# Strassen's seven products for the MLPs of a streaming encoder step

## The chip, the core and the metric

The kernel runs on one core of a Trainium2 chip. The metric is the device time of one execution in microseconds (us); lower is better. Three runs of the kernel before took 3055.25, 3056.92 and 3058.13 us. The engines are named as the profile does: PE is TensorE (matmuls), DVE is VectorE, ACT is ScalarE, POOL is GpSimd, and SP issues the DMAs.

## The reference

One step of a two-layer encoder: the first layer mixes tokens by a gated linear recurrence, the second by differential attention. Each layer ends in an MLP with a squared ReLU, and norms stand before and after each part. D is 1024, the hidden width 4096, and 1,152 tokens pass: 1,024 of a prompt and 128 of samples (8 streams of 16). All of it is fp32.

```python
def _rmsnorm(x, g):
    x32 = x.astype(jnp.float32)
    y = x32 * lax.rsqrt(jnp.mean(jnp.square(x32), axis=-1, keepdims=True) + NORM_EPS)
    return (y * g.astype(jnp.float32)).astype(x.dtype)

def _sqrelu_mlp(x, w_up, w_down):
    return jnp.square(jax.nn.relu(x @ w_up)) @ w_down
...
    for l in range(DEPTH):
        a = _rmsnorm(h, norm_g[l, 0])
...
        h = h + _rmsnorm(m, norm_g[l, 1])
        f = _sqrelu_mlp(_rmsnorm(h, norm_g[l, 2]), w_up[l], w_down[l])
        h = h + _rmsnorm(f, norm_g[l, 3])
```

## The kernel before

The 1,152 tokens are nine blocks of 128; blocks 0 to 7 are the prompt, block 8 the samples. Every large product is made of float32r pairs: an operand is split into a high part (a cast on ACT) and a low part (a subtraction on DVE), and `mm3` (L219) adds three matmuls, high by high, high by low and low by high. The normalised input of an MLP lies transposed in `aTh` and `aTl` for all nine blocks.

`out_proj` ends the mixing part: for each block in turn it adds to the residual h, takes the next norm and transposes the block (`to_aT`, four transposes into one PSUM bank, then ACT's cast and DVE's subtraction). The residual is kept in DRAM (`h_dr`).

`mlp` follows. The hidden width is 32 tiles of 128, taken in 15 groups of two or three. For each group, and for each of three groups of three token blocks, the up product `pu` is made (384 columns; L223 to L225), squared and split (L649 to L654), and then the down product `pd` of the token group before it (two halves of 512 columns in a PSUM tile of two banks) is added by DVE to an accumulator in SBUF (L618, one operation over both halves). The activations never leave SBUF. In the last group, `finish` (L622) loads h into one of three `hb` buffers, takes the norm, applies the gain on GpSimd (L629), adds (L631) and stores; in layer 0 it also takes the norm for attention and transposes.

PSUM has eight banks here: two tiles `mm`, two tiles `aux`, of a bank each, and two tiles `wide` of two banks. The order on each engine comes from a scheduler, except that the matmuls of the attention part are pinned in program order. An engine runs its instructions in that order, and each waits for semaphores of others.

Of the kernel before, what the change touches and what calls it, by code (L numbers as in the profile page):

```python
# [29 lines left out]
NFT = FF // P  # L30
EPS = 1e-6
LEVELS = (1, 2, 4, 8, 16, 32, 64)
# masked pieces of a block's scores: query offset, period and width, key range, column
# [9 lines left out]
POOL_MLP = {1, 2, 3, 4, 5, 6, 7, 8}  # L43
POOL_OUT = {4}
# attention schedule: work units between prompt steps, fill of its start, order of the parts of a step, sample parts
# [7 lines left out]
# last head: blocks whose output projection starts after a step, then the order of all blocks  # L53
# [10 lines left out]
def tile_kernel(ctx, tc, x_prompt, x_sample, cache_k, cache_v, state_hgrn, norm_g, w_hgrn_in,  # L64
# [16 lines left out]
    class Area:  # L81
        """A pool for each tag, in address order of the given tags, then of first use."""
# [6 lines left out]
        def pool(self, tag):  # L89
            if tag not in self.pools:  # L90
                self.pools[tag] = self.stack.enter_context(tc.tile_pool(name=f"{self.name}_{tag}", bufs=2, **self.kw))
            return self.pools[tag]
# [20 lines left out]
    h_dr = [dram.tile([T, D], F32, tag=f"h{i}", name=f"h_dr{i}") for i in range(3)]  # L113

    aTh = glob.tile([P, NB, KT, P], F32R, name="aTh")
    aTl = glob.tile([P, NB, KT, P], F32R, name="aTl")
    pre = ctx.enter_context(ExitStack())
# [14 lines left out]
    def load_w(src, a, n, gains=None, pool=None, sfx="", eng=None):  # L132
        """1024 elements a partition: DRAM to an exact float32r pair."""
        pool = pool or glob
        st = glob.tile([P, a, n], F32, tag="wst", name="wst", bufs=2)
# [27 lines left out]
    def rstd_of(ss, n, inv_d, pool, y=None):  # L163
        """(ss * inv_d + EPS) ** -0.5: root, reciprocal and a Newton step, scaled by powers of two."""
# [24 lines left out]

    def to_aT(a, b, psum=None, gain=None):  # L190
        """Token-major block a (SBUF) to columns of aT, times a gain of each row of a tile."""
# [17 lines left out]
    def pre_norm(h, g2, junk, dst, pool, b):  # L209
        """dst = rms-normalised h (times g2), then to aT."""  # L210
# [7 lines left out]
        to_aT(dst, b)  # L218
# [8 lines left out]
    def aT_blk(k, b):  # L227
        return aTh[:, b, k, :], aTl[:, b, k, :]
# [103 lines left out]
    with ExitStack() as hs:  # L332
# [11 lines left out]
        for h in range(H):  # L344
# [6 lines left out]
            for tg in range(NTG):  # L351
# [35 lines left out]
                # score products, level by level  # L387
# [39 lines left out]
                for c in range(3):  # L427
# [26 lines left out]
                    # token-major decayed keys  # L454
# [21 lines left out]
                    # o: sum of squares over the head, gate  # L476
# [5 lines left out]
                    # state  # L482
# [41 lines left out]
    def out_weights(w, js, gains, pp):  # L524
        """Units of an output projection: two row tiles of a half, the first half's four first."""
# [9 lines left out]
    def prepare(ob, b, o_src, osc, gain, pp):  # L535
        """Token block b of the heads' outputs, rms-normalised, to aT."""
# [11 lines left out]
    def out_proj(w, gains, gain, o_src, osc, g_post, h_old, h_new, g_pre, order, W=None, early={}):  # L548
        with ExitStack() as os_:
# [3 lines left out]

            def prep(b):
                if b not in early:
                    prepare(pp.tile([P, D], F32, name=f"ob{b % 2}", bufs=1), b, o_src, osc, gain, pp)
# [7 lines left out]
            g2 = bcast_gain(g_pre, pp, 2)  # L564
            for b in order:
# [7 lines left out]
                t = pp.tile([P, D], F32, name="t")  # L573
# [18 lines left out]
                pre_norm(hb, g2, t, t, pp, b)  # L592

# [1 line left out]
    def mlp(l, g_post, h_old, h_new, last):  # L595
# [4 lines left out]
        with ExitStack() as ms:  # L600
# [3 lines left out]
            def down(hT, wds, g, tg):  # L604
                for c in range(3):
# [13 lines left out]
                    if g == len(groups) - 1:  # L619
                        finish(b)  # L620
# [481 lines left out]
```

## Time and profile before

| | us |
|---|---|
| three runs, median | 3056.92 |
| profiled execution, span | 3055.4 |
| PE busy | 2990.4 (98%) |
| DVE busy | 1725.0 (56%) |
| ACT busy | 991.4 (32%) |
| POOL busy | 217.9 (7%) |

The span is the time of one profiled execution from its first to its last event; the busy times are how long each engine had an instruction in work, and they overlap. The stages lie so: start and recurrence to about 625 us, the first output projection to 746, MLP 0 to about 1545, attention to about 2150, its output projection to 2245, MLP 1 to about 3040, and the end.

### The profile page before, as it was taken

What the parts mean: (1) busy time and instruction counts of PE and PEld (TensorE: products, weight loads), DVE (VectorE), ACT (ScalarE), POOL (GpSimd) and SP (SyncE); (2) the same over time, 40 slices, a digit from 0 to 9 for tenths busy, and PEclk for the clock granted to TensorE, in tenths of its full rate; (3) what the DMA queues carried; (4) which work ended last, traced back from release to release, by engine and by line L of the source; (5) the groups of instructions that cost most, each with busy time, mean ns of one, the idle gap of its engine ahead of it and who ended that gap; (6) DMA issues with size and microseconds to landing.
All of it is one profiled execution on the core that took longest, in us unless ns stands there. A gap on an engine that the chain in (4) does not pass through costs nothing.

```text
span 3055.4 us, 45695 instructions
## 1 busy us (share of the span) xinstructions
PE 2990.4 (98%) x18273; PEld 2752.1 (90%) x18273; DVE 1725.0 (56%) x3418; ACT 991.4 (32%) x2376; POOL 217.9 (7%) x232
## 2 busy tenths in 40 slices
PE   7999999999999999999989999999999999999998
PEld 7999999978999999999979999997899999999997
DVE  7777777776344444444576565656653444444436
ACT  5333223333321211212254455556442212212112
POOL 1111111100000000000131020110100000000002
PEclk9999999999999999999999999999999999999999
DMA  4112121153111111111132121222431111111113
GB/s 133 52 51 58 52 58 52 58 191 111 42 41 43 42 42 42 42 42 44 61 128 75 52 85 54 69 75 64 159 117 42 42 42 42 42 42 48 36 35 110
DMA packets 227543, 199.73 MB, mean 65 GB/s; under 512 B 11865, under 2 KB 201474, under 8 KB 227330
## 3 DMA queue, kind: packets, MB, share of 16 engines
q1 hardware_dynamic: 227330, 196.81, 20.7%
q8 instruction: 144, 2.36, 0.3%
q14 instruction: 69, 0.57, 0.1%
HBM read 154.29 MB, written 42.47 MB: 64 GB/s over the span
## 4 chain that ended last, share of the span: by engine, by line
PE 92%; DVE 4%; ACT 2%; DMA 1%; issue 1%; SPq 0%; ACTq 0%; DVEq 0%
PE pj L738 9%; PE pu L223 9%; PE pu L225 9%; PE pu L224 9%; PE pd L224 8%; PE pd L225 8%; PE pd L223 8%; PE pi L223 2%; PE pi L224 2%; PE pi L225 2%; PE sc L738 2%; PE po L738 2%; PE pm L223 2%; PE pm L224 2%; PE pm L225 2%; PE pq L223 1%
## 5 line engine op out<-in xcount | busy, mean ns | idle before, releaser
L618 DVE TENSOR_TENSOR acc<-acc,pd 128x1024 f32<-128x1024 f32 x252 | 307.6, 1220 | 448.5 <-PE pd L225 448.5
L223 PE MATMUL pu<-aTh,whi 128*128 128x384 f32 x1536 | 515.4, 336 | 2.5 <-DVE aTl L206 1.8
L224 PE MATMUL pu<-aTl,whi 128*128 128x384 f32 x1536 | 514.9, 335 | 0.0
L225 PE MATMUL pu<-aTh,wlo 128*128 128x384 f32 x1536 | 514.9, 335 | 0.0
L224 PE MATMUL pd<-wlo,hh 128*128 128x512 f32 x1152 | 451.6, 392 | 0.0
L225 PE MATMUL pd<-whi,hh 128*128 128x512 f32 x1152 | 451.6, 392 | 0.0
L223 PE MATMUL pd<-whi,hh 128*128 128x512 f32 x1152 | 448.7, 390 | 1.7 <-DVE acc L618 1.7
L155 ACT CAST whi<-wst 128x1024 fp32r<-128x1024 f32 x192 | 199.0, 1051 | 603.0 <-PE pu L224 310.1
L156 DVE TENSOR_TENSOR wlo<-wst,whi 128x1024 fp32r<-128x1024 f32 x184 | 228.1, 1251 | 166.2 <-ACT whi L155 165.7
L224 PEld LDWEIGHTS pu<-aTl,whi 128*128 128x128 f32 x1536 | 288.4, 188 | 6.8
L223 PEld LDWEIGHTS pu<-aTh,whi 128*128 128x128 f32 x1536 | 288.3, 188 | 6.8 <-DVE aTl L206 2.0
L225 PEld LDWEIGHTS pu<-aTh,wlo 128*128 128x128 f32 x1536 | 288.3, 188 | 3.1
L225 PEld LDWEIGHTS pd<-whi,hh 128*128 128x128 f32 x1152 | 216.1, 188 | 45.4
L738 PE MATMUL pj<-whi,aTh 128*128 128x256 f32 x864 | 254.4, 294 | 1.9 <-DVE V L778 1.7
L223 PEld LDWEIGHTS pd<-whi,hh 128*128 128x128 f32 x1152 | 216.7, 188 | 43.4 <-DVE acc L618 2.5
L224 PEld LDWEIGHTS pd<-wlo,hh 128*128 128x128 f32 x1152 | 216.3, 188 | 41.7
L738 PE MATMUL pj<-wlo,aTh 128*128 128x256 f32 x864 | 244.9, 283 | 0.9 <-DVE wlo L156 0.9
L738 PE MATMUL pj<-whi,aTl 128*128 128x256 f32 x864 | 244.7, 283 | 0.0
L649 ACT ACTIVATE r<-pu 128x384 f32<-128x384 f32 x192 | 93.8, 489 | 414.7 <-PE pu L225 413.8
L650 DVE SCALAR_TENSOR_TENSOR r<-pu,r 128x384 f32<-128x384 f32 x192 | 106.2, 554 | 184.1 <-ACT r L649 183.8
L738 PEld LDWEIGHTS pj<-whi,aTh 128*128 128x128 f32 x864 | 165.7, 192 | 8.9 <-issue 4.5
L223 PE MATMUL pi<-whi,aTh 128*128 128x256 f32 x576 | 167.3, 290 | 1.1 <-ACT sf L365 1.1
(273 smaller groups left out, 5414.0 us busy)
## 6 DMA issues: line engine op xcount, KB each, us to landing
wst<-in_w_up_dram SPq DMA_DIRECT2D x64, 512.0 KB, 4.0
wst<-in_w_down_dram SPq DMA_DIRECT2D x64, 512.0 KB, 3.6
h_dr<-hb SPq DMA_DIRECT2D x27, 512.0 KB, 3.5
hb<-h_dr SPq DMA_DIRECT2D x27, 512.0 KB, 3.4
o_dr<-og SPq DMA_DIRECT2D x136, 64.0 KB, 1.7
wst<-in_w_hgrn_in_dram SPq DMA_DIRECT2D x16, 512.0 KB, 4.1
wst<-in_w_hgrn_in_dram SPq DMA_DIRECT2D x32, 256.0 KB, 3.0
wst<-in_w_kv_dram SPq DMA_DIRECT2D x32, 256.0 KB, 3.6
```

The source lines that it names most:

```text
L155: nc.scalar.copy(hi, st)
L156: (eng or nc.vector).tensor_tensor(out=lo, in0=st, in1=hi.bitcast(F32), op=ALU.subtract)
L223: matmul(out, lh, rh, start=first, stop=False)
L224: matmul(out, lh, rl, start=False, stop=False)
L225: matmul(out, ll, rh, start=False, stop=last)
L618: nc.vector.tensor_tensor(out=acc[b], in0=acc[b], in1=pd, op=ALU.add)
L649: nc.scalar.activation(r, pu[:, :TG], AF.Relu)
L650: nc.vector.scalar_tensor_tensor(out=r, in0=pu[:, :TG], scalar=0.0, in1=r, op0=ALU.max, op1=ALU.mult)
L738: pin(nc.tensor.matmul(*a, **k))
```

## The change

One level of Strassen's method (in Winograd's form) takes the place of the plain products for the eight prompt blocks: the operands are cut into 2 x 2 parts, seven products of sums of parts are made in place of eight, and the results are added up. Even blocks are the upper half of the tokens, odd blocks the lower; the inner width is cut in two.

- `mlp_up` has 16 iterations of two hidden tiles. Each makes P1 to P7 of 512 columns, four inner tiles by three matmuls each. P1 and P2 add up in one bank (`X`), P6, P7 and P4 in another (`Y`), P5 and P3 in half of a wide tile (`Z`). The other half of that wide tile takes the sample's product (`us`, 24 matmuls of 256 columns) and its transposes (`pt`). DVE adds u2, u3 and c22, c12, c21; ACT takes the ReLU; GpSimd squares, and the result goes to DRAM (`u_dr`, `us_dr`).
- The sums of the weights' parts are made on GpSimd (`sums`), those of the tokens' parts on GpSimd in `out_proj` (`pair_sums`); S1, S3 and S4 are transposed in the first iteration (`s_ops`), S2 takes the place of the odd blocks' first half in aT.
- `mlp_down` is a stage of its own, behind the whole of `mlp_up`. For each of 8 groups of four hidden tiles it loads the activations from DRAM, makes their sums and splits, and four token pairs by seven products of 512 columns; each product is added to its own accumulator by DVE (ACT copies in group 0). Six banks serve in turn, the last two being the halves of one wide tile. The samples' products add up in the other wide tile. Behind the last group `combine` adds the accumulators up, and `finish` works on two `hb` buffers.
- All PE work of the MLPs is pinned in program order. The weight rings are closed before an MLP and opened anew after it, pools take another mode of reuse, and `POOL_MLP` leaves GpSimd the gains of blocks 1, 3, 5, 7 and 8.

```diff
+            W = {"P1": ("A11", 0, 0, 0), "P2": ("A12", 0, 1, 0), "P3": ("S4", 0, 1, 1), "P4": ("A22", 1, 1, 0),
+                 "P5": ("S1", 1, 0, 0), "P6": ("S2", 1, 1, 1), "P7": ("S3", 1, 0, 1)}
...
+            for i in range(NFP):
...
+                X, Y, Wd = ps_mm("X"), ps_aux("Y"), ps_wide("Z")
+                Z, us, pt = Wd[:, 0:512], Wd[:, 512:768], Wd[:, 768:1024]
+                prod(X, "P1", sets, True, True)
...
+                nc.scalar.copy(p1, X)
+                if i == 0:
+                    s_ops("S1", lambda j: blk[2 * j + 1][:, 512:D])
+                sample_T(pend)
+                prod(Y, "P6", sets, True, True)
+                if i == 0:
+                    s_ops("S3", lambda j: blk[2 * j + 1][:, 0:512])
+                    s_ops("S4", lambda j: blk[2 * j][:, 512:D])
...
+                add(out=u2, in0=Y, in1=p1, op=ALU.add)
+                prod(Z, "P5", sets, True, True)
+                prod(X, "P2", sets, False, True)
...
+                nc.scalar.activation(c11, X, AF.Relu)
+                emit(c11, 0, i)
+                prod(Y, "P7", sets, False, True)
...
+                add(out=u3, in0=Y, in1=p1, op=ALU.add)
...
+                add(out=c22, in0=Z, in1=u3, op=ALU.add)
+                nc.scalar.activation(c22, c22, AF.Relu)
+                emit(c22, 3, i)
+                if nx is not None:
+                    raw = split(nx, 2 * i + 2)
+                    sums(nx)
+                wh, wl = sets[0]
+                for k in range(KT):
+                    mm3(us, aT_blk(k, NBP), (wh[:, k, :], wl[:, k, :]), k == 0, k == KT - 1, matmul)
...
+                nc.scalar.activation(hs, us, AF.Relu)
...
+                prod(Z, "P3", sets, False, True)
...
+                add(out=c12, in0=Z, in1=u2, op=ALU.add)
...
+                prod(Y, "P4", sets, False, True)
...
+                add(out=c21, in0=Y, in1=p1, op=ALU.add)
...
+            ORD = [("P1", "A11", "B11"), ("P5", "S1", "T1"), ("P7", "S3", "T3"), ("P6", "S2", "T2"),
+                   ("P2", "A12", "B21"), ("P3", "S4", "B22"), ("P4", "A22", "T4")]
...
+            def bank():
+                n = nb[0] % 6
+                nb[0] += 1
+                if n < 4:
+                    return (ps_aux if n % 2 else ps_mm)("pd")
+                if n == 4:
+                    wide[0] = ps_wide("pd")
+                return wide[0][:, (n - 4) * 512:(n - 3) * 512]
...
+                for q in range(2):
+                    mm3(o, (ah[:, q, c], al[:, q, c]), (bh[:, q], bl[:, q]), q == 0, q == 1, matmul)
+                a = ACC[p][:, j]
+                if g == 0:
+                    nc.scalar.copy(a, o)
+                else:
+                    nc.vector.tensor_tensor(out=a, in0=a, in1=o, op=ALU.add)
...
+                        combine(j)
+                        for p, an, bn in ORD[4:]:
+                            prod(g, p, an, bn, j)
+                        finish(2 * j, aE[:, :, j])
```

Where the instructions stand. In these rows a name ends in its buffer's number, and "waits" names the engine (or DMA queue) whose semaphore must have come first.

PE before, in the middle of MLP 0, where an up product gives way to the down product of the token group before (`pu_9560`, `pd_9546`; both halves of pd stand in line):
```order
L223 MATMUL pu_9560<-aTh_71,whi_9434 128x384
L224 MATMUL pu_9560<-aTl_72,whi_9434 128x384
L225 MATMUL pu_9560<-aTh_71,wlo_9435 128x384
...
L223 MATMUL pd_9546<-whi_9098,hh_9356 128x512 [waits DVE_49]
L224 MATMUL pd_9546<-wlo_9099,hh_9356 128x512
L225 MATMUL pd_9546<-whi_9098,hh_9356 128x512
```
Only the first of a down product's twelve matmuls waits there, and up matmuls stand on both sides of it.

PE of the change, in the second up iteration of MLP 0: the end of P7 (into `Y_9103`), the start and end of the sample's product and the start of P3 (both into the wide tile `Z_9104`):
```order
L218 MATMUL Y_9103<-a3h_8895,s0l_9080 128x512
L218 MATMUL Z_9104<-s2h_9025,aTh_81 128x256 [waits DVE_49]
L218 MATMUL Z_9104<-s2l_9026,aTh_81 128x256
...
L218 MATMUL Z_9104<-s2h_9025,aTl_82 128x256
L218 MATMUL Z_9104<-a4h_8925,s2h_9025 128x512 [waits Activation_49]
L218 MATMUL Z_9104<-a4l_8926,s2h_9025 128x512
```
DVE of the change, the same iteration, from u2 to c21:
```order
L763 TENSOR_TENSOR u2_9138<-Y_9103,p1_9117 128x512 [waits DVE_49,PE_49,Activation_49]
L771 TENSOR_TENSOR u3_9180<-Y_9103,p1_9117 128x512 [waits PE_49]
L773 TENSOR_TENSOR c_9182<-Z_9104,u3_9180 128x512 [waits DMAHW1_49,DVE_49]
L788 TENSOR_TENSOR c_9236<-Z_9104,u2_9138 128x512 [waits PE_49,DMAHW3_49,Activation_49,Pool_49]
L691 TENSOR_TENSOR s2l_9242<-wst0_9136,s2h_9241 128x1024 [waits Activation_49] x2
L795 TENSOR_TENSOR c_9259<-Y_9103,p1_9117 128x512 [waits DMAHW5_49,PE_49]
```
The sample's product now follows P7 at once and waits for DVE, whose c22 (`c_9182`) stands behind u3, which reads P7's bank; P3 waits for ACT.

DVE before, in MLP 0, around the accumulations of a token group (`acc0` to `acc2`):
```order
L654 TENSOR_TENSOR hh_10963<-r_10960,hh_10963 128x384 [waits Activation_49]
L618 TENSOR_TENSOR acc0_8930<-acc0_8930,pd_10966 128x1024 [waits PE_49]
L618 TENSOR_TENSOR acc1_8948<-acc1_8948,pd_10980 128x1024 [waits PE_49]
L618 TENSOR_TENSOR acc2_8966<-acc2_8966,pd_10994 128x1024 [waits PE_49]
L156 TENSOR_TENSOR wlo_11127<-wst_11124,whi_11126 128x1024 [waits DMAHW7_49,PE_49,Activation_49]
```
DVE of the change, in a middle down group, around the wide product tile `pd_12804`:
```order
L923 TENSOR_TENSOR a6_11608<-a6_11608,pd_12774 128x512 [waits PE_49]
L923 TENSOR_TENSOR a6_11608<-a6_11608,pd_12782 128x512 [waits PE_49]
L877 TENSOR_TENSOR w1l_12792<-wsta_12518,w1h_12791 128x1024 [waits Activation_49,Pool_49]
L923 TENSOR_TENSOR aE_11606<-aE_11606,pd_12804 128x512 [waits PE_49] x2
L923 TENSOR_TENSOR aE_11606<-aE_11606,pd_12819 128x512 [waits PE_49]
```
PE of the change, the two halves of that tile (the first row of each half, and what stands between):
```order
L218 MATMUL pd_12804<-w2h_12713,aTh_81 128x512 [waits DVE_49]
L218 MATMUL pd_12804<-w2l_12714,aTh_81 128x512
L218 MATMUL pd_12804<-w2h_12713,aTl_82 128x512 [waits Pool_49]
...
L218 MATMUL pd_12804<-w2h_12713,aTl_82 128x512 [waits Pool_49]
L218 MATMUL pd_12804<-w2h_12713,aTh_81 128x512 [waits DVE_49]
L218 MATMUL pd_12804<-w2l_12714,aTh_81 128x512
```
An accumulation now covers one half, a weight split (L877) stands ahead of the first half's, and the second half's first matmul waits for DVE, with nothing else on PE between the halves.

PE of the change, at the start of MLP 0, from the end of P6 to P5 (S3's and S4's transposes, `pt`; the four of a bank are two rows each):
```order
L218 MATMUL Y_8837<-aTh_81,s1l_8831 128x512
L215 MATMUL pt_8897<-ident_155,t_7731 128x128 [waits DVE_49]
L215 MATMUL pt_8904<-ident_155,t_7836 128x128 [waits DVE_49]
L215 MATMUL pt_8911<-ident_155,t_8070 128x128 [waits DVE_49]
...
L215 MATMUL pt_8948<-ident_155,t_8185 128x128 [waits DVE_49,Pool_49]
L218 MATMUL Z_8838<-a1h_8853,s1h_8830 128x512 [waits Activation_49]
```
PE before, the last block's transposes at the same point of the program (`pt_8639`, `pt_8646`), among the up matmuls:
```order
L223 MATMUL pu_8790<-aTh_71,whi_8768 128x384
L224 MATMUL pu_8790<-aTl_72,whi_8768 128x384
L196 MATMUL pt_8639<-ident_136,t_8612 128x128 [waits DVE_49,PE_49]
L196 MATMUL pt_8646<-ident_136,t_8612 128x128 [waits PE_49]
L225 MATMUL pu_8790<-aTh_71,wlo_8769 128x384
```
Before, up matmuls surround a block's transposes; now eight banks of transposes stand in one row, each waiting for DVE, and P5 behind them.

## Rows read from the trace of the kernel before

**Rows 1.** The page: the span, and the chain that ended last, by engine.
```profile
span 3055.4 us, 45695 instructions
...
PE 92%; DVE 4%; ACT 2%; DMA 1%; issue 1%; SPq 0%; ACTq 0%; DVEq 0%
```

**Rows 2.** Windows by stage: start:end, length, busy time of each engine, granted clock, DMA.
```profile
746.00:1515.00 769.00, 768.24 (x3905) 700.99 (x3905) 331.35 (x398) 170.79 (x276) 6.19 (x3) 1.00 0.14 44
1515.00:1600.00 85.00, 72.50 (x451) 64.88 (x450) 66.20 (x123) 49.43 (x99) 32.13 (x25) 0.96 0.43 138
2245.00:3015.00 770.00, 770.00 (x3918) 703.16 (x3918) 333.80 (x399) 167.75 (x273) 5.17 (x2) 1.00 0.15 44
```

**Rows 3.** The page's groups: instruction, tile, count | busy, mean ns | idle before.
```profile
L618 DVE TENSOR_TENSOR acc<-acc,pd 128x1024 f32<-128x1024 f32 x252 | 307.6, 1220 | 448.5 <-PE pd L225 448.5
...
L223 PE MATMUL pu<-aTh,whi 128*128 128x384 f32 x1536 | 515.4, 336 | 2.5 <-DVE aTl L206 1.8
...
L225 PE MATMUL pd<-whi,hh 128*128 128x512 f32 x1152 | 451.6, 392 | 0.0
```

**Rows 4.** Timeline of PE (start, length): first and last matmul of even runs; eight transposes.
```profile
1542.78 0.33 PE L223 MATMUL pu<-aTh,whi 128*128 128x384 f32 x1
...
1544.86 0.33 PE L223 MATMUL pu<-aTh,whi 128*128 128x384 f32 x1
...
1562.77 1.03 PE L196 MATMUL pt<-ident,acc 128*128 128x128 f32 x8
...
1566.15 0.39 PE L225 MATMUL pd<-whi,hh 128*128 128x512 f32 x1
...
1567.51 0.39 PE L225 MATMUL pd<-whi,hh 128*128 128x512 f32 x1
...
1570.62 0.28 PE L738 MATMUL pj<-whi,aTl 128*128 128x256 f32 x1
...
1571.93 0.28 PE L738 MATMUL pj<-wlo,aTh 128*128 128x256 f32 x1
```

**Rows 5.** Timeline of DVE and of PE: a weight split, and the matmul that waits for it.
```profile
1567.66 1.23 DVE L156 TENSOR_TENSOR wlo<-wst,whi 128x1024 fp32r<-128x1024 f32 x1 [0.25 <-ACT whi L155]
...
1568.94 0.39 PE L738 MATMUL pj<-wlo,aTh 128*128 128x256 f32 x1 [0.88 <-DVE wlo L156]
```

**Rows 6.** Groups by form: 512-element ACT cast and DVE subtraction from PSUM; GpSimd's 1,024 elements.
```profile
L206 DVE TENSOR_TENSOR aTl<-pt,aTh 128x512 fp32r<-128x512 f32 x90 | 58.9, 683 | 14.7 <-ACT aTh L205 14.7
...
L205 ACT CAST aTh<-pt 128x512 fp32r<-128x512 f32 x90 | 49.0, 587 | 43.7 <-PE pt L196 43.6
...
L629 POOL TENSOR_TENSOR acc<-acc,gb 128x1024 f32<-128x1024 f32 x16 | 39.0, 2438 | 885.1 <-ACT jk L182 885.1
```

**Rows 7.** Timeline of POOL and DVE around 1518, and the mean of that DVE operation.
```profile
1517.65 2.41 POOL L629 TENSOR_TENSOR acc<-acc,gb 128x1024 f32<-128x1024 f32 x1 [4.87 <-ACT jk L182]
...
1518.00 2.47 DVE L654 TENSOR_TENSOR hh<-r,hh 128x384 fp32r<-128x384 f32 x1 [0.25 <-ACT hh L653]
...
L654 DVE TENSOR_TENSOR hh<-r,hh 128x384 fp32r<-128x384 f32 x192 | 109.2, 570 | 92.4 <-ACT hh L653 92.2
```

**Rows 8.** Timeline of PE: two idles; the window behind the first, with its clock.
```profile
1534.03 0.50 PE L223 MATMUL pd<-whi,hh 128*128 128x512 f32 x1 [1.68 <-DVE acc L618]
...
1542.15 0.44 PE L223 MATMUL pu<-aTh,whi 128*128 128x384 f32 x1 [1.76 <-DVE aTl L206]
...
1535.00:1540.00 5.00, 4.98 (x27) 4.84 (x28) 3.93 (x7) 3.15 (x8) 0.89 (x1) 0.66 0.49 199
```

**Rows 9.** The end of the program: the last down matmul and the last DVE operation.
```profile
3040.25 0.39 PE L225 MATMUL pd<-whi,hh 128*128 128x512 f32 x1
...
3050.22 1.28 DVE L631 SCALAR_TENSOR_TENSOR hb<-acc,rs_y,hb 128x1024 f32<-128x1024 f32 x1
```

**Rows 10.** DMA issues: count, KB each, median us from issue to landing.
```profile
h_dr<-hb SPq DMA_DIRECT2D x27, 512.0 KB, 3.5
hb<-h_dr SPq DMA_DIRECT2D x27, 512.0 KB, 3.4
```

More of the change, by code (lines that the diff above doesn't have):

```diff
@@ L30 @@
 NFT = FF // P
+NFP = NFT // 2
+HT = NBP // 2 * P
 EPS = 1e-6
@@ L188, in bcast_gain, with pin, transpose, matmul @@
         return g
+    last = [None]
+    def pin(ins):
+        if last[0] is not None:
+            tc.add_manual_dep(ins.ins, last[0].name,
+                              mybir.DependencyInfo(mybir.DependencyClass.NoSync, mybir.DependencyReason.DATA),
+                              reason="order")
+        last[0] = ins.ins
+    def transpose(out, in_):
+        pin(nc.tensor.transpose(out, in_, ident))
+    def matmul(*a, **k):
+        pin(nc.tensor.matmul(*a, **k))
+    def half_T(src, hi, lo, tr=None):
+        tr = tr or (lambda o, i: nc.tensor.transpose(o, i, ident))
+        pt = ps_aux("pt").rearrange("p (k t) -> p k t", k=4)
+        for k in range(4):
+            tr(pt[:, k, :], src[:, k * P:(k + 1) * P])
+        nc.scalar.copy(hi, pt)
+        nc.vector.tensor_tensor(out=lo, in0=pt, in1=hi.bitcast(F32), op=ALU.subtract)
     def to_aT(a, b, psum=None, gain=None):
@@ L564, in out_proj @@
             g2 = bcast_gain(g_pre, pp, 2)
+            done = set()
             for b in order:
@@ L572, in out_proj @@
                     prep(todo.pop(0))
-                t = pp.tile([P, D], F32, name="t")
+                t = block(b) if b in early else blk[b]
                 if early.get(b) is not None:
@@ L662, in tile_kernel, with pair_sums @@
-    out_proj(w_hgrn_out[0], lambda kr: [gv[:, G_ON + 2 * kr + i:G_ON + 2 * kr + i + 1] for i in range(2)],
+                if b % 2 == 0:
+                    half_T(t[:, 0:512], aTh[:, b, 0:4], aTl[:, b, 0:4])
+                half_T(t[:, 512:D], aTh[:, b, 4:8], aTl[:, b, 4:8])
+                done.add(b)
+                if b < NBP and b ^ 1 in done:
+                    pair_sums(blk, b // 2)
+        return blk, keep
+    def pair_sums(blk, j):
+        e, o = blk[2 * j], blk[2 * j + 1]
+        a11, a12, a21, a22 = e[:, 0:512], e[:, 512:D], o[:, 0:512], o[:, 512:D]
+        tt = nc.gpsimd.tensor_tensor
+        tt(out=a22, in0=a21, in1=a22, op=ALU.add)
+        tt(out=a21, in0=a11, in1=a21, op=ALU.subtract)
+        tt(out=a11, in0=a22, in1=a11, op=ALU.subtract)
+        tt(out=a12, in0=a12, in1=a11, op=ALU.subtract)
+        half_T(a11, aTh[:, 2 * j + 1, 0:4], aTl[:, 2 * j + 1, 0:4])
@@ L815, in early_half @@
                 hold.append(ap.tile([P, 2, D], F32, name="KS0", bufs=1))
[L816 removed]
+                hold.extend(wr[0].tile([P, 2, 512], F32R, tag=t, name=t, bufs=NW) for t in ("whi", "wlo"))
             prepare(hold[0][:, b % 2, :], b, o_dr[1], scale_heads, gv[:, G_SUB:G_SUB + 1], ap)
```

367 lines of the change are left out of this document (283 added, 84 removed).

## The prediction

> **What bounds the kernel now.** I read the page first: its span and the chain that ended last [rows 1]. 92% of the span is TensorE (PE) on that chain, and the up products pu and the down products pd of the MLPs are the largest of its lines. Then the table of windows [rows 2]: in the two stretches in which only MLP work runs, PE is busy 768.2 of 769 us and 770.0 of 770 at a granted clock of 1.00. VectorE (DVE) has 331 to 334 us of work there, GpSimd (POOL) 5 to 6. So an MLP is paid in PE columns, and every microsecond for which PE waits in it is a microsecond of the result; PE waits for nobody there yet. The stretch behind MLP 0 is looser: PE is busy 72.5 of 85 us, 12.5 idle. Third, the timeline of PE for the price of one matmul [rows 4]: 512 columns follow each other in 1.36/6 = 0.227 us, 384 in 2.08/12 = 0.173, 256 in 1.31/11 = 0.119, and eight transposes take 1.03 us, so about (1.03 - 0.28)/7 = 0.107 each.
>
> **What the products save.** Per layer, half of the 4,608 pu and 3,456 pd matmuls (three lines of 1,536 and 1,152 each) [rows 3]: 2,304 x 0.173 + 1,728 x 0.227 = 399.3 + 391.7 = 791.0 us. After: 16 up iterations of 7 x 12 products of 512 columns and 24 sample matmuls of 256, 16 x (84 x 0.227 + 24 x 0.119) = 350.4; and 8 down groups of (28 + 4) x 6 matmuls of 512, 8 x 192 x 0.227 = 348.2. That is 698.6 a layer: **-92.4 a layer, -184.8 in all**. Only the prompt blocks lose an eighth, and the sample's 128 rows now pass alone, in 256-column and 512-column matmuls.
>
> **Transposes.** S1, S3 and S4 take 48 a layer, the sample's activations 32: 80 x 0.107 = 8.6 a layer, **+17.1**.
>
> **Waits inside an up iteration.** The sample product `us`, its transposes `pt` and P5/P3's `Z` are parts of one PSUM tile, and the order shows the first us matmul waiting for DVE and the first P3 matmul for ACT. By the numbers behind these waits, they are c22 (which reads Z) and the relu that reads us. DVE can start c22 only after u3, which needs P7's last matmul, the instruction just ahead of us on PE. Nothing else is queued on PE between them. The price: a 512-column matmul lasts 0.39 and the next could follow after 0.23, so 0.16 [rows 4]; an engine answers PE, and PE another, after about 0.05, since wlo ended at 1568.89 and pj started at 1568.94; that first matmul lasts 0.39 where a streamed one lasts 0.28, so 0.11 [rows 4, 5]; a DVE operation of 512 elements with a PSUM input takes 0.68 [rows 6]. u3 and c22: 0.16 + 0.05 + 0.68 + 0.05 + 0.68 + 0.05 + 0.11 = 1.78. The relu of 256 columns is not in the trace; ACT's 512-element cast takes 0.59 [rows 6], so it lies between 0 and 0.59, and I take 0.40, as an operation halved keeps more than half (DVE: 1.22 for 1,024, 0.68 for 512 [rows 3, 6]): 0.16 + 0.05 + 0.40 + 0.05 + 0.11 = 0.77. Together 2.55 x 32 iterations, **+81.6**. The weight splits and the sums on POOL (eight 512-element operations of about 1.2 in a 24-us iteration) stand in DVE's and POOL's order half an iteration ahead of their use, behind P3 and P1: nothing, as long as PE has those 24 us; were DVE 3 us late, P6 would wait for the rest.
>
> **Waits inside the down stage.** Products take six PSUM banks in turn; the last two are halves of one wide tile. The order has the second half's first matmul waiting for DVE (ACT in group 0), and what it waits for is the accumulation of the first half. This holds for 74 of the 448 products. Each costs 0.16 + 0.05 + 0.68 + 0.05 + 0.11 = 1.05, **+77.7**, provided that DVE is idle when the first half ends. The other four banks are four products ahead (5.4 us), which covers them.
>
> **DVE's queue in the down stage.** A group has 28 accumulations (19.0 us) and 12 splits of 1,024 elements (1.23 [rows 5]: 14.8) on DVE, 11 operations of 1,024 elements (2.44 each [rows 6]: 26.8) on POOL, against 43.6 + 4.9 of PE with the waits. So DVE is near its limit, and in 30 of the 74 places a split stands directly ahead of the accumulation that PE waits for. It starts when the accumulation before it ends, 0.9 us into a 1.36 us product, and ends 0.75 too late. What POOL adds is visible in before: a split of 384 elements that takes 0.57 lasted 2.47 when it started 0.35 us after a POOL operation, and ended with it [rows 7]. POOL is at work about half of the time here, so a split loses on average half of 2.44 with a chance of a half, 0.6. The bounds are 0 (POOL's gaps fall right) and 3.2 (0.75 and a whole POOL operation). I take 1.35 x 30 and a little carried on to the others: **+45**, between 0 and 110. The Trainium skill, page SBUF — State Buffer, section Who interferes with whom, has it that a DVE operation with two SBUF inputs and a GpSimd one that reads SBUF exclude each other for the whole instruction; the rows agree, and by it the accumulations, with one input in PSUM, stay at 0.68.
>
> **Start of each MLP.** Block 8's transposes now stand right behind P1 on PE's queue, with everything else pinned behind them. Its two norms are a chain as long as the one that ends the program (3040.6 to 3051.5 [rows 9], 10.9 us), which today runs beside pu products of other blocks. P1 covers 12 x 0.227 = 2.7, so about 8 idle. Behind P6, the eight transpositions for S3 and S4 share a single PSUM bank, as Y holds the other, so each waits for the DVE split of the last: 0.60 + 0.05 + 0.59 + 0.05 + 0.68 + 0.05 = 2.0, eight times 16, of which 3.4 is counted as transposes: 12 more. S1's four add 1 or so. **+42** for both layers, between 20 (half of the chain hidden) and 50.
>
> **From MLP 0 to attention.** Nine blocks are finished through two hb buffers instead of three, and a buffer's turn is a load (3.4), the final operation (1.28) and the store (3.5) [rows 9, 10], 8.2 us. The ninth's turn comes four turns after the first's, 33 us. Counted from where the last group's P6 ends, the first final operation comes at about 9 (12 products' third, 4.1, then square sum, gain and root), the ninth at 42, and its norm and transposes are done at 48. PE has 72 matmuls of 0.227 there and 72 transposes, 24 us, so 24 idle instead of 12.5; the order puts the first pj behind the transposes of all nine blocks. Less the waits counted already (4), and with the query weights that then load one after another (3.4 + 2.4 + 1.2 + 1.2 = 8) and a lower clock after idling: **+25**, between 5 and 45. **End of the program:** the same two buffers without norms: the ninth block's final operation ends at 43 and its store 4 later; PE's 72 matmuls and four waits end at about 20.5, so 26.5 instead of 15 (3040.3 to 3055.4 [rows 1, 9]): **+11.5**.
>
> **Sum.** 3055.4 - 184.8 + 17.1 + 81.6 + 77.7 + 45 + 42 + 25 + 11.5 = 3170.5 in the profile's terms. The median of the runs shown, 3056.92, is 1.5 above that profile's span: **3172**, slower by 3.8%.
>
> **The rivals.** *The waits are short: faster.* The gain and the transposes leave 167.7 to spend, and the boundaries (42 + 25 + 11.5) take 78.5 of it. If PE's waits inside the two stages cost under 89 us in all instead of 81.6 + 77.7 + 45 = 204, so less than half, the kernel is faster; with none it ends at 2968. For it: the boundaries are short, and each wait is for one instruction. Against it: 0.68 is what every 512-element DVE operation with a PSUM input took, and the up iteration has two in a row. Chance 0.10.
> *The clock falls at each wait.* In before, PE idled 1.68 us ahead of 1534.03, and the 5 us from 1535 on ran at a mean clock of 0.66 of full speed (1.2 GHz for part, 2.4 for the rest) [rows 8]: 1.7 us lost. After the idle of 1.76 at 1542.15 the matmuls kept their 0.173 [rows 4, 8]. If each up iteration lost 1.5 so, +48: 3220. The page TensorE: Matmul & The Clock Gate of the Trainium skill, section A second HAM failure mode, tells of a kernel whose PSUM banks in rotation made PE idle often enough for the clock to swing; the two idles here disagree on it. Chance 0.12.
> *DVE and POOL set the pace of the down stage.* If each of the 12 splits waited for a whole POOL operation, DVE's group would be 19 + 12 x 3.7 = 63 us against 51 for PE with its waits: 16 x 12 = 190 more than with a DVE that keeps up, in place of my 45: 3317. POOL's gaps speak against it. Chance 0.06.
> *The waits stand, the rest is hidden:* no queue on DVE and half of the boundaries, 3172 - 45 - 39 = 3088. Chance 0.12.
>
> **Numbers.** The forecast itself gets 0.60; its own range is 3110 to 3215. For 8 in 10 the range takes in the hidden case and the clock: 3085 to 3255. A change within 0.2%, about 6 us, is what a measurement of this kernel can't tell from none; no case ends there, 0.02 for it. Faster 0.10, slower 0.88.
>
> **What would show it.** In the changed profile, 32 idles of about 1.8 us ahead of us with DVE c22 (L773) as releaser and 32 of 0.8 ahead of P3 with ACT hs; 74 idles of 1.05 and more ahead of pd, released by acc at L923; split rows (L877, L845) above 1.23 in the mean; some 20 us idle around each MLP's first iteration; a tail of 26 us. If pd or us follow at 0.23 without a wait, the first rival is true; if matmuls of 512 columns are 0.43 apart after the waits, the clock; if POOL is busy over 80% in the down stage, the third. What would prove me wrong beyond these is an up or down window whose PE busy time is not 350 or 348.

## The result and the profile after

The changed kernel takes 3366.14 us (four runs, 3364.57 to 3368.29) against 3056.16, a ratio of 1.101 with a 95% interval of 1.0996 to 1.1028: slower by 10%, where 3172 was forecast and 3255 was the upper end of the range. The sign was right, the size was not.

The page of the kernel after, the span and the engines' line:

```profile
span 3363.0 us, 44867 instructions
...
PE 2955.6 (88%) x16897; PEld 2535.5 (75%) x16897; DVE 1976.7 (59%) x3604; ACT 1198.1 (36%) x2536; POOL 1117.2 (33%) x746
```

PE is idle for 407 us (3363.0 - 2955.6), where it was idle for 65 in the span of before [rows 1]. The product work is down by about what was forecast, but busy time counts a matmul's length, which grows when the clock falls, so it hides that here. The table of windows shows where the time goes (columns: stretch, length, busy time of PE, PEld, DVE, ACT, POOL, granted clock, DMA share, GB/s):

```profile
761.00:808.00 47.00, 25.10 (x94) 18.39 (x93) 22.00 (x30) 14.31 (x25) 13.05 (x8) 0.63 0.18 56
808.00:1209.00 401.00, 365.14 (x1732) 297.34 (x1732) 135.86 (x144) 121.29 (x176) 191.09 (x144) 0.99 0.28 91
1209.00:1224.00 15.00, 4.19 (x12) 2.65 (x11) 7.20 (x5) 6.35 (x8) 12.80 (x7) 0.64 0.69 243
1224.00:1640.00 416.00, 359.70 (x1462) 281.92 (x1460) 277.20 (x287) 129.01 (x145) 216.81 (x89) 0.96 0.23 74
1640.00:1713.00 73.00, 35.05 (x111) 25.73 (x109) 49.60 (x89) 30.06 (x57) 16.70 (x8) 0.66 0.27 90
1713.00:1800.00 87.00, 66.68 (x493) 64.20 (x493) 39.03 (x93) 37.37 (x78) 20.95 (x23) 0.81 0.28 88
3302.00:3363.00 61.00, 21.75 (x74) 16.19 (x72) 44.51 (x72) 12.75 (x28) 18.18 (x8) 0.70 0.39 138
```

The reader is to set these beside [rows 2]. The even stretches, 808 to 1209 (up) and 1224 to 1640 (down), have PE at work for 91% and 86% of the time at a clock of 0.99 and 0.96. The edges are worse: the first up iteration (761 to 808), the change from up to down (1209 to 1224), and the last group with the nine finishes (from 1640 on) have PE at work for about half of the time or less, at a clock of 0.63 to 0.66. The waits of PE, grouped by what it waited for (us in all, times, longest):

```profile
PE Z L218 <- DVE c L773: 55.0, 32, 4.1
...
PE pd L218 <- DVE a L923: 49.8, 28, 3.5
...
PE pd L218 <- DVE aO L923: 48.0, 22, 5.2
...
PE pt L222 <- ACT aO L253: 26.1, 4, 8.2
...
PE pd L218 <- DVE aE L923: 23.8, 16, 2.6
...
PE smp L218 <- ACT aTh L886: 21.3, 2, 10.7
...
PE pt L235 <- DVE t L578: 20.4, 2, 13.4
...
PE Z L218 <- ACT hs L783: 16.8, 32, 0.5
...
PE pt L222 <- POOL t L656: 16.1, 2, 9.1
```

The two waits that the forecast is built on are there: 32 for c22 and 32 for hs (71.8 us idle; with the restarts 81.6 was forecast), and 66 for DVE's accumulation of a half (121.6 us idle; 77.7 + 45 was forecast for 74 with their restarts, of which ACT releases eight). The others, 16 to 26 us each, stand at the edges. One iteration in the timeline of PE (start, length, and in brackets the idle time ahead):

```profile
1017.96 0.40 PE L218 MATMUL Y<-a3h,s2l 128*128 128x512 f32 x1
...
1019.92 0.39 PE L218 MATMUL Z<-s1h,aTh 128*128 128x256 f32 x1 [1.56 <-DVE c L773]
...
1022.74 0.28 PE L218 MATMUL Z<-s1h,aTl 128*128 128x256 f32 x1
...
1023.55 0.50 PE L218 MATMUL Z<-a4h,s1h 128*128 128x512 f32 x1 [0.53 <-ACT hs L783]
```

P7's last matmul starts at 1017.96; the sample's first would follow at 1018.19 and starts at 1019.92. P3 follows the sample's last by 0.81 instead of 0.12. Thirty such iterations took 25.15 us each, from P7 to P7; 24.66 was forecast (21.90, two transposes of 0.107 and 2.55 of waits). In the down stage, from the same view:

```profile
1406.18 0.39 PE L218 MATMUL pd<-w0h,aTl 128*128 128x512 f32 x1
...
1409.37 0.50 PE L218 MATMUL pd<-w0h,aTh 128*128 128x512 f32 x1 [2.80 <-DVE a L923]
...
1418.92 0.40 PE L218 MATMUL pd<-w2h,aTl 128*128 128x512 f32 x1
...
1421.87 0.79 PE L218 MATMUL pd<-w2h,aTh 128*128 128x512 f32 x1 [2.56 <-DVE aE L923]
...
1422.46 0.63 PE L218 MATMUL pd<-w2l,aTh 128*128 128x512 f32 x1
1422.89 0.63 PE L218 MATMUL pd<-w2h,aTl 128*128 128x512 f32 x1
```

Between halves lie 3.2 and 2.95 us here, and after the second the matmuls last 0.63 and follow at 0.43: the clock is at 1.2 GHz for a while. A group took 55.1 us (the mean from the first product of the first group to that of the eighth); 51.2 was forecast. The groups of instructions behind it:

```profile
L923 DVE TENSOR_TENSOR a<-a,pd 128x512 f32<-128x512 f32 x168 | 112.3, 682 | 76.3 <-PE pd L218 76.1
...
L877 DVE TENSOR_TENSOR w0l<-wsta,w0h 128x1024 fp32r<-128x1024 f32 x34 | 62.5, 1839 | 18.3 <-ACT w0h L876 18.3
...
L877 DVE TENSOR_TENSOR w0l<-wstb,w0h 128x1024 fp32r<-128x1024 f32 x10 | 25.2, 2516 | 6.2 <-ACT w0h L876 6.2
...
L845 POOL TENSOR_TENSOR aTl<-hst,aTh 128x1024 fp32r<-128x1024 f32 x48 | 120.9, 2521 | 88.2 <-ACT aTh L844 88.2
...
L830 POOL TENSOR_TENSOR hst<-hst 128x1024 f32<-128x1024 f32 x16 | 50.2, 3140 | 27.9 <-DVE aTl L845 27.9
...
L835 POOL TENSOR_TENSOR hst<-hst 128x1024 f32<-128x1024 f32 x16 | 38.3, 2391 | 39.3 <-DVE aTl L845 39.3
```

An accumulation, with one input in PSUM, keeps its 0.68. A split with both inputs in SBUF takes 1.47 to 2.52 in the mean of its row, 1.75 over all 192, instead of 1.23 [rows 5]. GpSimd's own sums take 2.38 to 3.14, where its gain took 2.44 [rows 6].

### The profile page after: what moved, and what is told of

It is laid out like the page before. It is cut to its first block, busy times and chain, and to the rows that moved or that the text cites. A ratio compares the mean times of both kernels' runs of the same rounds, so it can differ in the third digit from the quotient of the medians.

```text
span 3363.0 us, 44867 instructions
## 1 busy us (share of the span) xinstructions
PE 2955.6 (88%) x16897; PEld 2535.5 (75%) x16897; DVE 1976.7 (59%) x3604; ACT 1198.1 (36%) x2536; POOL 1117.2 (33%) x746
## 5 line engine op out<-in xcount | busy, mean ns | idle before, releaser
L725 POOL TENSOR_TENSOR c<-c 128x512 f32<-128x512 f32 x128 | 184.4, 1440 | 348.6 <-ACT c L789 147.7
L218 PE MATMUL pd<-w2h,aTh 128*128 128x512 f32 x304 | 131.8, 434 | 48.8 <-DVE aO L923 17.5
L262 PE MATMUL pi<-wlo,aTh 128*128 128x256 f32 x576 | 166.1, 288 | 0.0
L218 PEld LDWEIGHTS pj<-wlo,aTh 128*128 128x128 f32 x864 | 164.7, 191 | 1.8 <-DVE wlo L170 1.1
L263 PE MATMUL pi<-whi,aTl 128*128 128x256 f32 x576 | 165.4, 287 | 0.0
L218 PE MATMUL pd<-w1h,aTh 128*128 128x512 f32 x288 | 121.6, 422 | 49.6 <-DVE aO L923 25.1
L218 PEld LDWEIGHTS pj<-whi,aTl 128*128 128x128 f32 x864 | 164.4, 190 | 0.0
L218 PE MATMUL pd<-w0h,aTh 128*128 128x512 f32 x304 | 124.3, 409 | 32.1 <-DVE a L923 18.9
L218 PE MATMUL pd<-w2h,aTl 128*128 128x512 f32 x304 | 127.8, 420 | 0.0
L218 PE MATMUL pd<-w2l,aTh 128*128 128x512 f32 x304 | 127.8, 420 | 0.0
```

The lines of the kernel that those rows point to most:

```text
L218: pin(nc.tensor.matmul(*a, **k))
L262: matmul(out, lh, rl, start=False, stop=False)
L263: matmul(out, ll, rh, start=False, stop=last)
L725: nc.gpsimd.tensor_tensor(out=c, in0=c, in1=c, op=ALU.mult)
```

## Experiments

The single edits and the first two combinations were run once each. Stages that an edit leaves alone differ by 3 to 4 us between these runs (MLP 1 with the end took 941.8 us in the changed kernel, 938.5 and 938.4 in two runs whose edits lie ahead of it), so a gain below 10 us is read from the waits and not from the time alone.

**The waits inside the stages.** First the sample's own PSUM tile in the up stage:

```diff
-                Z, us, pt = Wd[:, 0:512], Wd[:, 512:768], Wd[:, 768:1024]
+                Z = Wd[:, 0:512]
...
+                Ud = ps_wide("us")
+                us, pt = Ud[:, 0:256], Ud[:, 256:512]
```

> Only the up stage changes: the sample's product and its transposes get a wide PSUM tile of their own, so they no longer share one with P5 and P3. Theory A (PE is the bound and each wait on the shared tile is paid in full): the 55 us behind DVE c22 and the 17 us behind ACT hs disappear, with some 0.1 us of restart for each of 64, so about 80 us less: 3285 us. Theory B (DVE, ACT and GpSimd set the pace of an up iteration and the shared tile only shows it): PE waits elsewhere in the iteration instead, and no more than 30 us are gained: 3335 or more.

Measured: 3275.2 us, 91 less. An iteration takes 22.51 us instead of 25.15; its products and two transposes alone were worked out at 19.04 + 2.86 + 0.21 = 22.11. Both waits are gone, and nothing took their place; the 0.40 that is left over lies in the distance of the matmuls, 0.231 to 0.234 us in the mean for 512 columns, not 0.227. Theory A.

Then five banks, each a tile of its own (the fifth is half of a wide tile whose other half stays unused), in the down stage:

```diff
-                n = nb[0] % 6
+                n = nb[0] % 5
...
-                if n == 4:
-                    wide[0] = ps_wide("pd")
-                return wide[0][:, (n - 4) * 512:(n - 3) * 512]
+                return ps_wide("pd")[:, 0:512]
```

> Only the down stage changes: five PSUM banks in turn, each a tile of its own, in place of four and two halves of a wide tile. Theory A (the wait between the halves is the loss): the 62 waits of 122 us in all disappear, the clock of 0.96 in the down stage returns to nearly 1, about 140 us less: 3225 us. Theory B (DVE and GpSimd, which exclude each other, set the pace of the down stage): PE then waits at the next reuse of a bank instead, and no more than 40 us are gained: 3325 or more.

Measured: 3220.3 us, 146 less; a group takes 44.3 us instead of 55.1. A window in the middle of that stage:

```profile
1230.00:1540.00 310.00, 310.00 (x1351) 253.36 (x1350) 248.12 (x263) 122.15 (x136) 215.86 (x79) 1.00 0.28 93
```

PE is at work all the time at a clock of 1.00, beside DVE at 80% and POOL at 70%. DVE and GpSimd did not set the pace: the splits are as long there as before (1.42 to 2.58 us in the mean by row), but with five banks in turn PE doesn't wait for them. Theory A. One thing got worse: from the last sample product of MLP 0 to the run of attention's products 116 us pass, 99 in the changed kernel.

To price the long splits, the down stage without the eight sums a group on GpSimd; three of them here, and the other five likewise:

```diff
                     x, y, z = hst["A11"], hst["A21"], hst["A22"]
-                    gp(out=x, in0=x, in1=y, op=ALU.subtract)
-                    gp(out=y, in0=y, in1=z, op=ALU.add)
                     hst["S3"], hst["S1"] = x, y
...
-                    gp(out=x, in0=hst["A22"], in1=x, op=ALU.subtract)
```

> The down stage without its eight sums a group on GpSimd (operands are split as they are loaded, so the products are of unsummed parts); GpSimd keeps three splits a group. Theory A: DVE's splits fall from means of 1.5 to 2.5 us to about 1.25, and the wait between halves from 1.9 us to some 1.1, so about 50 us less: 3315 us. Theory B: DVE and GpSimd no longer collide, the down stage runs at PE's pace, 100 us or more less: 3265 or below.

Measured: 3328.7 us, 37 less; a group takes 52.7 us instead of 55.1. The waits of PE:

```profile
PE pd L218 <- DVE aO L915: 38.2, 22, 5.1
...
PE pd L218 <- DVE a L915: 32.0, 28, 1.6
...
PE pd L218 <- DVE aE L915: 23.2, 16, 2.3
```

They fall from 121.6 to 93.4 us. That is nearer to theory A, and theory B fell. So the sums are worth about a quarter of the wait between the halves. The splits fell from 1.75 to 1.56 us in the mean over all 192, not to 1.25 as theory A had it, as three splits a group stay on GpSimd: what all of the collision is worth, no run shows.

Both PSUM edits together:

> The first two edits together (a wide tile of its own for the sample in the up stage, five single banks in the down stage). Theory A: the gains add, about 220 us less: 3145 us, still above the kernel before (3056). Theory B: 3290 or more.

Measured: 3135.8 us, 230 less, where the two had given 91 and 146 alone. They add but for 7 us. What is left, 79 us above the kernel before, lies at the edges.

**The edges, one by one.** S3's and S4's transposes ahead of the tile Y, so that they have both banks:

```diff
                     s_ops("S1", lambda j: blk[2 * j + 1][:, 512:D])
+                    s_ops("S3", lambda j: blk[2 * j + 1][:, 0:512])
+                    s_ops("S4", lambda j: blk[2 * j][:, 512:D])
                 sample_T(pend)
+                Y = ps_aux("Y")
                 prod(Y, "P6", sets, True, True)
-                if i == 0:
-                    s_ops("S3", lambda j: blk[2 * j + 1][:, 0:512])
-                    s_ops("S4", lambda j: blk[2 * j][:, 512:D])
```

> Only the first up iteration of each MLP changes: S3 and S4 are transposed right behind S1, before the bank Y is taken, so that the transposes have two banks in turn instead of one. Theory A (one bank makes each transpose wait for DVE's split of the last): of the 20 us of such waits in both layers most disappear, with the clock about 25 us less: 3342 us. Rival (the stage waits for GpSimd's sums and the norms of the last blocks anyway, so the wait only moves): within 6 us of 3366.

Measured: 3343.4 us, 23 less, theory A.

The buffers hb, from the four of the activations' loads:

```diff
-                hb = R.tile([P, 2, 512], F32, name="hb", bufs=2)
+                hb = L.tile([P, 2, HT], F32, tag="hst", name="hb", bufs=4)
```

> Only the end of each MLP changes: hb takes the four buffers of the activations' loads, which are free by then, instead of two of its own. Theory A (the turn of two buffers, load, last operation, store, sets the pace of the nine finishes): from the last group's end to the end of the program 61 us become 45, from MLP 0 to attention 97 become 70, about 43 us less: 3323 us. Rival (ACT's and DVE's order, one block behind the other, sets the pace): 3355 or more.

Measured: 3352.0 us, 14 less. It is all at the end of the program: from the last sample product to the end 47 us instead of 61, where theory A had 45. Ahead of attention 95 us were measured instead of 99, where it had a gain of 27: something else sets the pace of the finishes there.

The first sample product behind P1's products:

```diff
-                    if bn[0] == "B":
+                    if bn[0] == "B" and (g or bn != "B11"):
...
                             prod(g, p, an, bn, j)
+                        if g == 0:
+                            sample(g, bn)
```

> Only the first down group changes: its P1 products stand ahead of the first sample product instead of behind it. Theory A (the 10.6 us idle between the stages is the way of the last sample tile through DRAM, which the prompt products do not need): four products of 1.36 us move into the idle time, 11 us less in both layers: 3355 us. Rival (the prompt's activations come back from DRAM as late): within 4 us of 3366.

Measured: 3348.9 us, 17 less; PE's wait for the sample's split falls from 10.65 to 5.5 us a layer. From the last P4 to the second group the two layers gain 9 us together; where the other 8 lie, this edge doesn't explain. Theory A.

All five, and the move of the statistics tiles:

> All five edits (own wide tile for the sample, five single banks, two banks for S3 and S4, four hb buffers, P1 ahead of the first sample product), and the small statistics tiles of the first output projection moved in memory, away from the last store of the sample states. Theory A (each wait is paid by itself): 3136 of the two edits measured together, less 25, 43, 11 and 8: 3049 us, level with the kernel before. Rival (the waits behind these take their place): 3110 or more.

Measured: 3098.3 us, between the two: 37 less than with the two edits, where the other four gave 63 one by one (23, 14, 17 and, in a run further down, 9). The waits of PE in this run:

```profile
PE pt L222 <- ACT aE L253: 46.6, 4, 18.1
...
PE pt L222 <- ACT aO L253: 20.6, 4, 6.7
```

A single wait of 18.1 us, for the copy (L253) of a finished block ahead of its transposes. On PE these transposes stand ahead of the next pair's down products, so the products wait for a chain of two norms. That is what the buffers had not changed, and it is longer with five banks, 116 us as in the run with them alone; why, no run shows. The edit that follows from it, alone:

```diff
-                    for c in range(2):
-                        half_T(y[:, c], aTh[:, b, 4 * c:4 * c + 4], aTl[:, b, 4 * c:4 * c + 4])
+                    later.append((b, y))
...
             finish(NBP, a1[:, 0:2])
+            for b, y in later:
+                for c in range(2):
+                    half_T(y[:, c], aTh[:, b, 4 * c:4 * c + 4], aTl[:, b, 4 * c:4 * c + 4])
```

> Only the end of MLP 0 changes: the transposes of the nine finished blocks are written behind all nine finishes, so that none stands ahead of a down product on PE. Theory A (PE's order puts a block's transposes ahead of the next pair's products, so products wait for a chain of two norms of some 18 us, three times): the 97 us between the last group and attention become about 60, 35 us less: 3331 us. Rival (the two hb buffers set the pace of the nine finishes, whatever PE does): 3358 or more.

Measured: 3348.7 us, 17 less: a part of that edge, 87 us instead of 99, not the whole. The products no longer wait for transposes, but the nine last operations still follow each other at 7.7 us in the mean (9.2 in the changed kernel). Neither theory holds whole: the time lies between the two, and with four buffers, in the next combination, the mean is 7.6, so the buffers don't set it.

The statistics tiles of the first output projection alone (the order string of its memory begins with "ss ss8 rs_v rs_y rs_t"):

> Only the memory order of the first output projection changes: its small statistics tiles no longer lie where the sample states of the last head are stored from. Theory A (the 13.4 us idle ahead of the first output projection's transposes is DVE waiting for that store): 5 to 13 us less: 3357 us. Rival (the loads of the first blocks, late behind the first load of the up weights on SP's queue, set it): within 3 us of 3366.

Measured: 3357.1 us, 9 less. PE's wait falls from 13.4 to 6.1 us. Gone is DVE's wait for the store, which the changed kernel shows so:

```profile
641.43 0.32 DVE L183 TENSOR_SCALAR rs_v<-ssh 128x8 f32<-128x8 f32 x3 [8.24 <-DMA out_dram<-Ss]
```

So a good half of the 13.4 was that store. What is left ends with a load (DVE idle for 3.49 us, released by t<-o_dr). But the first product starts at 641.7 instead of 647.0 and MLP 0 only at 760.3 instead of 761.7: most of the 9 us lies behind this stage, where nothing was changed, and is not shown to be its gain.

**Together.** With the transposes moved, the last pair's sums on DVE, and P2 behind P1:

```diff
-        tt = nc.gpsimd.tensor_tensor
+        tt = (nc.vector if j == 3 else nc.gpsimd).tensor_tensor
...
                 if i == 0:
+                    prod(X, "P2", sets, False, True)
                     s_ops("S1", lambda j: blk[2 * j + 1][:, 512:D])
```

> All edits (3098 us in the run of six), and the transposes of MLP 0's finished blocks behind its products, the last pair's sums on DVE instead of GpSimd, P2 right behind P1 in the first iteration. Theory A (each wait is paid by itself): 3098 less 45 less 10: 3043 us, 0.5% faster than the kernel before. Rival (the finishes take as long wherever the transposes stand): 3085 us or more, slower than before.

Measured: 3071.9 us, a ratio of 1.0048 (1.0031 to 1.0064): 26 less than the run of six edits, where 55 were expected: between theory A and the rival. In its timeline, DVE, ACT and POOL between two finishes in MLP 0:

```profile
1534.98 1.28 DVE L952 SCALAR_TENSOR_TENSOR hb<-aE,rs_y,hb 128x1024 f32<-128x1024 f32 x1
...
1536.35 1.06 ACT L196 ACTIVATE jk<-hb 128x1024 bf16<-128x1024 f32 x1 [0.52 <-DVE hb L952]
...
1537.87 1.06 ACT L196 ACTIVATE jk<-aO 128x1024 bf16<-128x1024 f32 x1
...
1539.15 2.34 POOL L950 TENSOR_TENSOR aO<-aO,gb 128x1024 f32<-128x1024 f32 x1 [12.16 <-ACT rs_y L184]
...
1539.34 2.16 DVE L187 SCALAR_TENSOR_TENSOR rs_t<-rs_y,rs_v 128x1 f32<-128x1 f32 x1
...
1542.78 1.28 DVE L952 SCALAR_TENSOR_TENSOR hb<-aO,rs_y,hb 128x1024 f32<-128x1024 f32 x1
```

The reader is to follow one block. DVE's last operation of a block ends at 1536.26; ACT then takes that block's square sum for the next norm (1536.35), and only behind it the square sum of the block that follows (1537.87). Its gain on GpSimd begins at 1539.15, a DVE operation on one column waits out that gain (2.16 us), and the next block's last operation comes at 1542.78: 7.8 us a block, with four buffers free. So the order on ACT and the gain on GpSimd are the chain that the rows show. The last run therefore writes a block's square sum and gain ahead of the block before it, takes the gains to DVE, and has three more edits, which its expectation names:

```diff
+            def finish(b, y):
+                first(b, y)
+                if len(ready) > 1:
+                    second(*ready.pop(0))
...
-POOL_MLP = {1, 3, 5, 7, 8}
+POOL_MLP = set()
```

> All edits of the run before (3072 us), and five at the edges of the stages: each block's sum of squares and gain are written one block ahead of the last operation of the block before, all gains are on DVE, block 8 is transposed behind S4 instead of ahead of S1, the first sample tile is split behind the first prompt tiles, and the second output projection's statistics tiles are moved as the first's. Theory A (what is left are chains at the edges of the stages, and each is paid by itself): nine finishes at 5.5 instead of 7.5 us before attention (18), 5 at the end, 6 at each start, 5 at each change from up to down, 3 ahead of the second projection, 48 us in all: 3024 us, 1% faster than the kernel before. Rival (the chains are bound by work of ACT and DVE that no order takes away): 3057 or more, no faster than before.

Measured: 3041.8 us (3039.75 to 3045.6), a ratio of 0.9950 to the kernel before (0.9936 to 0.9963): faster by half a percent, and by 9.6% than the changed kernel; 18 us short of the expectation. The nine last operations ahead of attention now start between 1522.6 and 1559.2, 4.6 us apart in the mean and in pairs, where the run before had 7.6; order and gains were moved together, so which of the two did it stays open. The profiled executions of the two runs are 29 us apart, and all of it lies between the start of MLP 0 and the second output projection, whose wait for its first transposes (7.0 in the changed kernel) is gone. The edits at the start and at the change from up to down brought nothing: from the first P1 to the first P7 MLP 0 takes 40.3 us instead of 40.1 and MLP 1 44.8 instead of 38.8. The page's span and windows:

```profile
span 3040.1 us, 44824 instructions
```

```profile
757.00:800.00 43.00, 26.80 (x121) 20.09 (x120) 26.41 (x36) 16.80 (x28) 9.45 (x7) 0.85 0.22 68
800.00:1130.00 330.00, 330.00 (x1618) 275.59 (x1617) 121.84 (x133) 111.64 (x163) 172.05 (x134) 1.00 0.31 99
1130.00:1170.00 40.00, 29.76 (x128) 23.10 (x127) 21.55 (x14) 16.28 (x22) 31.56 (x15) 0.86 0.53 176
1170.00:1480.00 310.00, 310.00 (x1345) 253.24 (x1345) 251.15 (x261) 121.67 (x135) 224.49 (x81) 1.00 0.32 101
1480.00:1590.00 110.00, 75.98 (x364) 63.51 (x364) 88.01 (x171) 56.17 (x100) 34.76 (x28) 0.75 0.34 112
```

The even stretches are now like those of before [rows 2]: 330.0 of 330 and 310.0 of 310, at 1.00. What PE still loses in this layer, 16, 10 and 34 us, lies in the first, third and fifth row, at the edges.

## Why the prediction was wrong

**Products (-184.8).** Near. With the waits gone an up iteration took 22.51 us for 22.11 and a group in the middle of the down stage 44.1 for 43.5: matmuls of 512 columns followed each other at 0.229 to 0.234 us in the mean, not at the 0.227 of one run [rows 4]. The kernel before was priced as low (over its MLPs the means are 0.174 and 0.229 us), so the two errors nearly cancel: by the means about 176 of the 184.8 were saved (estimate).

**Waits in an up iteration (+81.6).** Right: 32 x (25.15 - 22.51) = 84 by the iterations, 91 by the run without them.

**Wait between the halves and DVE's queue (+77.7 and +45).** The mechanism was right, the size too small: 55.1 - 44.3 = 10.8 us a group instead of 7.7. In fourteen groups that is 151 us, where the forecast's terms hold 107, and the run without the waits gave back 146. PE idled for 106 of the 151 (the forecast's terms, less their restarts, hold 90); the other 45 are restarts and matmuls that follow more slowly at a mean clock of 0.96, where 17 were counted for restarts and nothing for the clock. That is the part that was mis-sized most. The rival in which the clock falls at each wait was placed in the up stage, where it stayed at 0.99; it came in the down stage, where waits reach 2.5 to 3.5 us. The third rival's 3317 is the number nearest to the result, but its mechanism fell: without the wait, PE is at work all the time beside the same DVE and POOL.

**Start of each MLP (+42).** The idle time was nearly right, the rest was not: the first iterations took 66.3 and 69.3 us, 75 more than two even ones and their 96 transposes. The rows of PE in the first of them:

```profile
772.06 1.11 PE L222 MATMUL pt<-ident,t 128*128 128x128 f32 x4 [6.98 <-POOL t L656]
...
776.50 1.94 PE L222 MATMUL pt<-ident,t 128*128 128x128 f32 x8 [3.33 <-DVE t L255]
...
791.68 0.66 PE L215 MATMUL pt<-ident,t 128*128 128x128 f32 x4 [1.40 <-DVE a3l L227]
```

Beside its ordinary waits PE idles for 22 and 24 us there, and 21 was forecast. Two thirds of the wait that was put down to block 8's norms are GpSimd's sums of the last pair, though (6.98 of 10.3, 9.1 of 12.8), which the forecast doesn't name. And all of it runs at a clock of 0.63: four transposes last 1.11 us, not 0.60. That was not counted.

**From up to down (nothing).** This is the first step that failed: the forecast has no term for it. The last sample tile goes to DRAM and back, and its product stands first on PE's queue, pinned. It cost 12.7 us a layer (14.1 between the last P4 and the first pd, less six matmuls):

```profile
1220.25 0.79 PE L218 MATMUL smp<-w0h,aTh 128*128 128x512 f32 x1 [10.63 <-ACT aTh L886]
```

The last up iteration lost another 4 us a layer, as its wait for c22 is 4.1 us long.

**From MLP 0 to attention (+25).** The second step that failed, and the largest: "a buffer's turn is a load (3.4), the final operation (1.28) and the store (3.5)", four turns for nine blocks. From the end of the last group's P6 the ninth block's transposes were done at 102 us (1636.7 to 1738.7), not at 48, and the two buffers were not what set it: four brought 4 us. PE's order puts a pair's transposes ahead of the next pair's products (up to 18.1 us of wait once the other waits were gone), and ACT's order puts one block's square sum behind the last operation of the block before it, so blocks followed each other one by one, not two by two, at 7.6 us in the mean, and at 4.6 once that order and the gains were changed. Up to the second output projection this stretch cost about 65 us by difference, 25 were forecast; 7.0 of it are a wait at that projection. At the end of the program the two buffers did matter: from the end of P6 to the end 63 us passed (3299.6 to 3363.0), 47 were forecast, and four buffers gave 14 back.

**The first output projection (nothing).** The forecast took the projections as unchanged. Its first transposes came 13.4 us late, behind a store from memory that the new layout gave to the statistics tiles, and behind loads; MLP 0 starts 15 us later than before (761.7 for 746.3):

```profile
645.26 1.11 PE L235 MATMUL pt<-ident,t 128*128 128x128 f32 x4 [13.40 <-DVE t L578]
```

**The account.** Forecast 3170.5, measured 3363.0 in the profile's terms, 192.5 apart, in rounded differences of measured and forecast (estimates, with the matmuls at their means): products 9, even up iterations 3, first iterations 33, last iterations and the change from up to down 34, even down groups 47, first projection 15, from the last group of MLP 0 to the second projection 40, the last group of MLP 1 and the end 13. Some 70% of it lie at the edges, where the forecast summed chains by their lengths, left out the order in which the engines take them, and counted full clock. The hidden rival and the faster one fell as well.

## What to carry to other kernels

Where a stage keeps PE full, an edit pays there what the count of columns says; what it cost here lies where PE must wait for another engine between two instructions that nothing separates, and at the edges of stages. Parts of one PSUM tile that different engines read at different times should be tiles of their own: that alone was worth 230 of the 310 us. Gains at edges don't add as these did: 63 us one by one were 37 together. Splitting a loop into two stages adds an edge each time, and each edge has to be followed on every queue in order, ACT's and SP's too.

## What the runs showed of the hardware

The clock was lower where PE waited longer, not where it waited more often. In the up stage, with 1.56 and 0.53 us of idle time in each 25.15 us, it stayed at 0.99. In the down stage, with as many waits (4.6 in 55.1 us), but 1.7 us long in the mean and up to 3.5, and with PE at work for 86% of the time, it was 0.96. With PE at work for about half of the time, in pieces, it was 0.63 to 0.66. Whether the length of a wait or the share of idle time decides, these runs don't separate. The Trainium skill, page TensorE: Matmul & The Clock Gate, section A second HAM failure mode, tells of a kernel whose turns through PSUM banks left PE short idles often enough for the clock to swing; by that the down stage agrees (0.96) and the up stage doesn't (0.99). Taking the waits away brought it back to 1.00 in both stages.

DVE's splits of 1,024 elements, with two inputs in SBUF, took 1.75 us in the mean beside GpSimd's work, 1.23 [rows 5] in before; its accumulations, with one input in PSUM, stayed at 0.68. GpSimd's operations of 1,024 elements took 2.38 to 3.14 by row, 2.44 [rows 6] in before; whether the longer ones waited for DVE is not shown. A short operation on DVE can be held as well: the one on a single column (L187) that began 0.19 us into a gain on GpSimd lasted 2.16 us and ended with it.
